# RWKV-7 time mixing: a pair's decays and scaled operands made at the end of the preceding block, and the next pair's projections ahead of the gate and v

## The chip, the cores and the metric

The kernel runs on one core of one Trainium2 chip, as one launch. The metric is the device time of that launch in microseconds, from runs on the chip; a profile was taken of one further execution. PE, DVE, ACT, POOL and SP are the core's engines for matmuls, for elementwise work, for activations, for general work and for issuing transfers; PEld is PE's loading of weights, which overlaps its matmuls.

## The reference

One inference step of a trunk with two layers, D = 1024, for a prompt of 256 tokens and for eight samples of four tokens. Layer 0 mixes tokens with Mamba-2, layer 1 with RWKV-7. What matters here is the RWKV-7 mixer:

```python
def rwkv7_mixer(u, S0, shift0, ...):
    xx = u_prev - u                                    # token shift
    xr, xw, xk, xv, xa, xg = u + xx * mu[i]            # six mixes
    r, k, v = xr @ w_r, xk @ w_k, xv @ w_v             # 1024 x 1024 each
    w = -softplus(-(w0 + tanh(xw @ w1) @ w2)) - 0.5
    a = sigmoid(a0 + (xa @ a1) @ a2)
    g = sigmoid(xg @ g1) @ g2
    kk = k * k_k, normalised per head;  k = k * (1 + (a - 1) * k_a)
    decay = exp(-exp(w))
    def step(S, inp):                                  # 16 heads of 64
        sa = S @ (-kk_t)
        S = S * d_t + sa (x) (kk_t * a_t) + v_t (x) k_t
        return S, S @ r_t
    y = groupnorm(y per head) * gn_w + gn_b + (sum(r * k * r_k) * v)
    return (y * g) @ w_o, S_new, ...
```

All of it is in float32, with the states of the recurrence as further outputs.

## The kernel before, in words

Activations lie feature-major: a tile is [128 features, 288 tokens], the 256 of the prompt and the 32 of the samples, and eight tiles are one row of 1024 features. A float32 product by a large weight is made as three matmuls (`mm3`: L147, L148, L149): weight and activation are each split into a high and a low part (`whi`, `wlo` in L55 and L56 for weights; L138 and L156, the helper `hilo`, for activations), and high x high, high x low and low x high are summed in one bank of PSUM. Weights come as 512 KB units of eight 128 x 128 tiles through two streams whose order is that in which the code asks for tiles: `ws`, whose tiles are split, and `wn`, whose tiles are used whole, as float32, by plain matmuls (L1053 in the lead, L1082 for the gate, L1132 for k). Such a matmul shows in the profile as two records.

The stage of the RWKV mixer lies at about 979 to 1300 us. Its 16 heads are worked in eight pairs (`KD = 8`), a pair being one tile of 128 features. After `lead` (norm, token shift, first half of the decays) and `bulk(0)` (projections of pair 0) it runs nine blocks, p = 0 to 8. In a block three sequences of steps are drawn in turns:

- `chain(p-1)`, in blocks 1 to 8: the recurrence of the pair before. It opens with the bonus (L1372 to L1384, two matmuls by `ones_m` in L1187 and L1188), goes through four chunks of 64 tokens and the samples in steps `solve` (L1393 to L1404), `solved` (L1409, L1410) and `state` (L1421 to L1429), and ends with the group norm, the bonus and the gate (L1470 to L1488).
- `prep(p)`, in blocks 0 to 7: the scaled operands of pair p and the inverse that `chain` needs. It has 18 steps. The first two make the decays `E1`, `E2` and `Ex` from a scan over the logarithms (L1229), the normalised key (a sum of squares by the matmuls L1187 and L1188), and the products `AR` and `BK`, which are r, k and kk times decays, padded for the samples (L1209, L1211). They begin with the load of the samples' state, `S0`, 256 KB, on SP. The third step multiplies BK by AR (L1263) and masks the result (L1269) into `AA`; the others transpose BK, and build the inverse by doubling levels (L1307 on PE, L1323 on DVE), X0, R (L1354) and TT (L1358).
- `fill(p)`: projections. `gates` (block 0 only) is the gate's first half, 16 matmuls L1082. `bulk2(p)` is the gate's second half and the v projection of pair p, with its transposes (L1178). `bulk(p+1)` is what pair p+1 needs first: sw and sa (L1098, L1099, each with a sigmoid that starts in L1119), the k projection (eight L1132) and the r projection (24 matmuls of `mm3`). In block 0 each projection also makes its mixes (L1105), and for r and v their splits. In blocks 7 and 8 come output projections (`wo`), of which `EARLY = 3` are begun in block 7.

Per round, each of `chain` and `prep` does one step and `fill` does `RATE` of its steps on average. This sets the program order. The scheduler that builds the instruction streams starts from that order and moves what its own estimate of times finds ready, so an engine's order is not the code's; the pieces of order below are what it makes of either code.

PSUM has eight banks, dealt out in rings: `main` is banks 0, 1 and 7, for projections; `A` is banks 2 and 3, for `prep` and the transposes of v; `R` is 4 and 5 and `Y` is 6, for `chain`. The products of L1263 write two banks of A for one pair of masks, and then two more for the transposes of BK. `AR` exists twice, by the parity of p; `BK` once.

After the blocks, the last of the eight terms of every output projection is added, which needs the last pair's y.

Of the kernel before, what the change touches and what calls it, by code (L numbers as in the profile page):

```python
# [16 lines left out]
KD = 8  # L17
# [8 lines left out]
class Stream:  # L26
# [34 lines left out]
    def next(self, name, kt, mt):  # L61
        self.order.append((name, kt, mt))
        self.ahead(self.k.la_split, self.k.la_units)
        i, o = divmod(self.used, PT)
        hi, lo = self.pieces[i]
        self.used += 1
        return hi[:, o * P:(o + 1) * P], lo[:, o * P:(o + 1) * P]
# [878 lines left out]


KAPPA = float(np.exp(-0.5))
RATE = 1.45
EARLY = 3  # L950
LEVELS = (1, 2, 4, 8, 16, 32)

# [539 lines left out]
def rwkv(k, g, g_next):  # L1492
    k.side = 0
    nc, ws = k.nc, k.ws
    r = k.r_next
    with k.tc.tile_pool(name="rwkv", bufs=1) as pool:
        k.wn.pool, k.wn.bufs = pool, 2
        w = Rwkv(k, pool)
        k.set_rings(main=[0, 1, 2, 3, 4, 5, 6, 7])
        w.lead(g, r)  # L1500
        w.consts()
        w.pads()
        k.set_rings(main=[0, 1, 7], A=[2, 3], R=[4, 5], Y=[6])
        for _ in w.bulk(0):
            pass
        k.renew(40, 48, F32)
        w.yg = k.A[40:48]
        ys = {}

        def wo(mo, kts):  # L1510

            ps = k.bank("main")[:, :NT]
            for i, kt in enumerate(kts):
                if kt not in ys:
                    ys[kt] = k.A[2 * kt], k.A[2 * kt + 1]
                    k.hilo(*ys[kt], w.yg[kt])
                k.mm3(ps, ws.next("r_wo", kt, mo), ys[kt], i == 0, i == len(kts) - 1)
                yield
            nc.vector.tensor_tensor(k.h[mo], k.h[mo], ps, ALU.add)

        def fill(p):

            if p == 0:
                yield from w.gates()
            if p < KD:
                yield from w.bulk2(p)
            if p + 1 < KD:
                yield from w.bulk(p + 1)
            if p == KD - 1:
                k.renew(0, 16)  # L1530
                for mo in range(EARLY):
                    yield from wo(mo, range(KD - 2))
            if p == KD:
                k.set_rings(main=[0, 1, 2, 3, 7], R=[4, 5], Y=[6])
                for mo in range(EARLY, KD):
                    yield from wo(mo, range(KD - 1))
                for mo in range(EARLY):
                    yield from wo(mo, [KD - 2])

        for p in range(KD + 1):  # L1540
            gens, acc = [], 0.0
            bulk = fill(p)
            if p < KD:
                gens.append(w.prep(p))
            if p > 0:
                gens.insert(0, w.chain(p - 1))
            while gens:
                for q in list(gens):
                    if next(q, "end") == "end":
                        gens.remove(q)  # L1550
                acc += RATE
                while acc >= 1:
                    acc -= 1
                    next(bulk, None)
            for _ in bulk:
                pass
        k.set_rings(main=[0, 1, 2, 3, 4, 5], aux=[6, 7])
        last = [wo(mo, [KD - 1]) for mo in range(KD)]
        for i in last[:6]:
            next(i)  # L1560
        k.side = 1
        k.renew(32, 48)
        for mo in range(KD):
            next(last[mo], None)
            if mo + 6 < KD:
                next(last[mo + 6])
            k.h_done(mo, g_next)
# [186 lines left out]
```

## Time and profile before

| | |
|---|---|
| runs | 1545.33, 1544.91, 1544.76 us; median 1544.91 |
| profiled execution | 1545.45 us, span of the trace 1543.6 us |
| instructions in the trace | 35587, of them 14178 matmul records on PE |
| mean granted clock of PE | 0.997 |
| L147, L148, L149 on activations and split weights | 2760 records each, 825.0, 819.0 and 814.9 us busy |
| L1132, k projections | 128 records, 40.8 us |
| L1323, masks of the inverse's levels | 40 instructions, 17.5 us of DVE |
| loads of `S0` | 8, of 256 KB, 3.7 us from issue to landing |

A page of the profile has busy times of the engines over the whole span, the chain of work that ended last, followed back from the last instruction, and groups of equal instructions with their count, busy time, mean and the idle time just ahead of them. Matmuls are pipelined, so a record's duration is longer than the distance to the next one; where the prediction speaks of the pace of matmuls, it takes distances of starts. The granted clock is a share of PE's full clock.

### The profile page before, as it was taken

What the parts mean: (1) busy time and instruction counts of PE and PEld (TensorE: products, weight loads), DVE (VectorE), ACT (ScalarE), POOL (GpSimd) and SP (SyncE); (2) the same over time, 40 slices, a digit from 0 to 9 for tenths busy, and PEclk for the clock granted to TensorE, in tenths of its full rate; (3) what the DMA queues carried; (4) which work ended last, traced back from release to release, by engine and by line L of the source; (5) the groups of instructions that cost most, each with busy time, mean ns of one, the idle gap of its engine ahead of it and who ended that gap; (6) DMA issues with size and microseconds to landing.
All of it is one profiled execution on the core that took longest, in us unless ns stands there. A gap on an engine that the chain in (4) does not pass through costs nothing.

```text
span 1543.6 us, 35587 instructions
## 1 busy us (share of the span) xinstructions
PE 1524.0 (99%) x14178; PEld 1422.4 (92%) x14178; DVE 1099.9 (71%) x2321; ACT 972.9 (63%) x2217; POOL 46.0 (3%) x143
## 2 busy tenths in 40 slices
PE   9999999999999999999999999999999999999997
PEld 8999998989989999999999999777777778999997
DVE  7666578888888766656876655887766778666566
ACT  7555458989887655554755554766666746555545
POOL 0000003112100000000000000100000000000000
PEclk9999999999999999999999999999999999999999
DMA  7555563765665555555555555531222224555551
GB/s 245 168 169 166 164 213 116 248 221 198 228 223 197 171 166 165 166 168 171 161 170 168 168 164 164 178 109 59 78 84 65 63 72 153 170 168 165 164 168 57
DMA packets 75574, 243.48 MB, mean 158 GB/s; under 512 B 11728, under 2 KB 16976, under 8 KB 75408
## 3 DMA queue, kind: packets, MB, share of 16 engines
q1 hardware_dynamic: 75408, 241.21, 48.6%
q8 instruction: 111, 1.82, 0.5%
q14 instruction: 55, 0.45, 0.1%
HBM read 226.54 MB, written 14.64 MB: 156 GB/s over the span
## 4 chain that ended last, share of the span: by engine, by line
PE 93%; DVE 4%; DMA 1%; ACT 1%; issue 1%; SPq 0%; POOL 0%; DVEq 0%; POOLq 0%; ACTq 0%
PE bank L147 26%; PE bank L149 26%; PE bank L148 25%; PE bank L1307 2%; PE bank L1132 1%; PE bank L770 1%; PE bank L1449 1%; PE bank L1421 1%; PE bank L774 1%; PE bank L766 1%; PE bank L641 1%; PE bank L1187 1%; DVE wlo L56 1%; PE bank L1381 1%; PE bank L1082 0%
## 5 line engine op out<-in xcount | busy, mean ns | idle before, releaser
L147 PE MATMUL bank<-act,whi 128*128 128x288 f32 x2760 | 825.0, 300 | 6.2 <-ACT act L138 3.7
L148 PE MATMUL bank<-act,whi 128*128 128x288 f32 x2760 | 819.0, 297 | 1.3 <-DVE act L156 1.3
L149 PE MATMUL bank<-act,wlo 128*128 128x288 f32 x2760 | 814.9, 296 | 0.1
L55 ACT ACTIVATE whi<-raw 128x512 fp32r<-128x512 f32 x754 | 472.1, 631 | 434.6 <-PE bank L148 421.9
L56 DVE TENSOR_TENSOR wlo<-raw,whi 128x512 fp32r<-128x512 f32 x754 | 515.2, 689 | 263.5 <-ACT whi L55 236.6
L147 PEld LDWEIGHTS bank<-act,whi 128*128 128x128 f32 x2760 | 517.2, 188 | 15.1 <-ACT act L138 5.2
L148 PEld LDWEIGHTS bank<-act,whi 128*128 128x128 f32 x2760 | 521.6, 189 | 6.4 <-DVE act L156 2.1
L149 PEld LDWEIGHTS bank<-act,wlo 128*128 128x128 f32 x2760 | 520.9, 189 | 3.0 <-DVE wlo L56 0.3
L147 PE MATMUL bank<-more,whi 128*128 128x288 f32 x192 | 56.7, 295 | 0.0
L148 PE MATMUL bank<-more,whi 128*128 128x288 f32 x192 | 56.4, 294 | 0.0
L149 PE MATMUL bank<-more,wlo 128*128 128x288 f32 x192 | 56.4, 294 | 0.0
L321 DVE TENSOR_TENSOR t<-bank,rstd 128x288 f32<-128x288 f32 x88 | 39.8, 456 | 23.0 <-PE bank L149 23.0
L324 DVE TENSOR_TENSOR u<-bank,s 128x288 f32<-128x288 f32 x88 | 39.8, 456 | 22.7 <-PE bank L149 22.6
L671 DVE SCALAR_TENSOR_TENSOR conv_a<-X,vec,conv_a 128x312 f32<-128x312 f32 x96 | 50.9, 534 | 2.6 <-ACT conv_a L138 2.2
L138 ACT ACTIVATE s<-t 128x288 f32<-128x288 f32 x104 | 45.8, 443 | 6.2 <-DVE t L366 3.5
L138 ACT ACTIVATE X<-bank 128x256 f32<-128x256 f32 (+2 forms) x98 | 30.5, 338 | 21.8 <-PE bank L1307 20.8
L138 ACT ACTIVATE act<-h,vec 128x288 fp32r<-128x288 f32 (+1 forms) x71 | 37.1, 528 | 7.3 <-DMA h<-in_xT 2.7
L1132 PE MATMUL bank<-act,raw 128*128 128x288 f32 x128 | 40.8, 434 | 0.0
L148 PEld LDWEIGHTS bank<-more,whi 128*128 128x128 f32 x192 | 36.3, 189 | 0.0
L149 PEld LDWEIGHTS bank<-more,wlo 128*128 128x128 f32 x192 | 36.2, 189 | 0.0
L147 PEld LDWEIGHTS bank<-more,whi 128*128 128x128 f32 x192 | 36.0, 187 | 0.0
L1323 DVE TENSOR_TENSOR Z<-bank,lv 128x256 f16<-128x256 f32 (+1 forms) x40 | 17.5, 437 | 24.1 <-PE bank L1307 23.5
(383 smaller groups left out, 1736.8 us busy)
## 6 DMA issues: line engine op xcount, KB each, us to landing
raw<-in_w SPq DMA_DIRECT2D x377, 512.0 KB, 3.6
h0a<-in_ssm_a SPq DMA_DIRECT2D x16, 512.0 KB, 5.4
h0b<-in_ssm_b SPq DMA_DIRECT2D x16, 512.0 KB, 5.1
out_ssm_s<-h0b SPq DMA_DIRECT2D x16, 512.0 KB, 3.9
raw<-in_wn SPq DMA_DIRECT2D x11, 512.0 KB, 3.6
S<-in_wkv_in SPq DMA_DIRECT2D x8, 256.0 KB, 3.7
out_wkv_s<-S SPq DMA_DIRECT2D x8, 256.0 KB, 2.0
h<-in_xT SPq DMA_DIRECT2D x8, 144.0 KB, 4.6
```

What stands on the lines that cost most here:

```text
L55: nc.scalar.activation(hi, src, AF.Copy)
L56: nc.vector.tensor_tensor(lo, src, hi.bitcast(F32), ALU.subtract)
L138: i = self.nc.scalar.activation(out, in_, func, **kw)
L147: nc.tensor.matmul(ps, wh, xh, start=start, stop=False)
L148: nc.tensor.matmul(ps, wh, xl, start=False, stop=False)
L149: nc.tensor.matmul(ps, wl, xh, start=False, stop=stop)
L321: nc.vector.tensor_tensor(t, pg, r, ALU.mult)
L324: nc.vector.tensor_tensor(u, pu, s, ALU.mult)
L671: nc.vector.scalar_tensor_tensor(a[:, :312], X[:, t:t + 312], k.g(f"conv_w{t}")[:, ct:ct + 1], a[:, :312], ALU.mult, ALU.add)
L1132: self.nc.tensor.matmul(ps, k.wn.next_whole("r_wk", kt, p), x[kt], start=kt == 0, stop=kt == KD - 1)
L1307: nc.tensor.matmul(ps[rows, ch], lhs(ch)[rows], rhs(ch)[rows], start=True, stop=True)
L1323: nc.vector.tensor_tensor(Z[:, :n], pz, lv(i, n), ALU.mult)
```

## The change

`fill` draws `bulk(p+1)` first, then in block 0 the gates, then `bulk2(p)`. `prep(p+1)` is begun in block p: as soon as `prep(p)` has ended and the r projection of pair p+1 exists (more of `fill` is drawn until it does), its first two steps run (`SCALES = 2`), and block p+1 goes on with its third. `RATE` goes from 1.45 to 1.65.

```diff
-RATE = 1.45
+RATE = 1.65
+SCALES = 2
...
         def fill(p):
 
+            if p + 1 < KD:
+                yield from w.bulk(p + 1)
             if p == 0:
                 yield from w.gates()
             if p < KD:
                 yield from w.bulk2(p)
-            if p + 1 < KD:
-                yield from w.bulk(p + 1)
...
+        def solve(p, bulk):
+
+            if p < KD:
+                yield from preps[p]
+            if p + 1 < KD:
+                while "r" not in w.d.get(p + 1, {}):
+                    next(bulk)
+                preps[p + 1] = w.prep(p + 1)
+                for _ in range(SCALES):
+                    next(preps[p + 1])
+                    yield
+
+        preps = {0: w.prep(0)}
         for p in range(KD + 1):
             gens, acc = [], 0.0
             bulk = fill(p)
-            if p < KD:
-                gens.append(w.prep(p))
+            gens.append(solve(p, bulk))
             if p > 0:
                 gens.insert(0, w.chain(p - 1))
```

Behind this place every line number is larger by one in the changed kernel: L1263 is L1264 there. No engine that computes gets more or fewer instructions; SP has one fewer, 1001 for 1002.

Four places show how the order of the engines changes. A row is a line of the code, an operation, what it writes and reads with the buffers' numbers, the shape, and how many such instructions follow one another.

PE in block 0, ahead of the first products of pair 0 (the first L1263). Before, `bank_1275` is the r projection of pair 0, `bank_1303` and `bank_1304` are the gate, `bank_1385` is sw of pair 1:

```order
L149 MATMUL bank_1275_13655<-act_1267_13611,wlo_13355 128x288
L147 MATMUL bank_1275_13655<-act_1268_13612,whi_13354 128x288
L1082 MATMUL bank_1303_13754<-mg_13781,raw_13480 128x288
L148 MATMUL bank_1275_13655<-act_1205_13441,whi_13354 128x288
L149 MATMUL bank_1275_13655<-act_1268_13612,wlo_13355 128x288
L1082 MATMUL bank_1304_13755<-mg_13781,raw_13480 128x288
L1098 MATMUL bank_1385_14155<-lw_13458,whi_13681 128x288
L1099 MATMUL bank_1385_14155<-lw_13458,wlo_13682 128x288
L1082 MATMUL bank_1303_13754<-mg_13807,raw_13480 128x288
L1082 MATMUL bank_1304_13755<-mg_13807,raw_13480 128x288
L1187 MATMUL bank_1402_14278<-ch_14279,ones_m_13570 128x288
L1263 MATMUL bank_1312_13787<-AR_1249_13589,BK_13591 64x128
```

In the changed order `bank_1329` is the r projection of pair 1, `bank_1310` its k projection (whose L1132 is now L1133), and the gate's matmuls come behind:

```order
L147 MATMUL bank_1329_13914<-act_1263_13607,whi_13378 128x288
L148 MATMUL bank_1329_13914<-act_1200_13436,whi_13378 128x288
L149 MATMUL bank_1329_13914<-act_1263_13607,wlo_13379 128x288
L147 MATMUL bank_1329_13914<-act_1264_13608,whi_13378 128x288
L1133 MATMUL bank_1310_13789<-act_1253_13597,raw_13480 128x288
L1133 MATMUL bank_1310_13789<-act_1254_13598,raw_13480 128x288
L1133 MATMUL bank_1310_13789<-act_1255_13599,raw_13480 128x288
L1133 MATMUL bank_1310_13789<-act_1256_13600,raw_13480 128x288
L1133 MATMUL bank_1310_13789<-act_1257_13601,raw_13480 128x288
L1264 MATMUL bank_1313_13796<-AR_1249_13589,BK_13591 64x128
L1264 MATMUL bank_1314_13797<-AR_1249_13589,BK_13591 64x128
```

What moved: the gate's L1082 are gone from here, and projections of pair 1 stand in their place.

PE in block 4, from the last products of BK and AR (ring A, both banks) to the next products that need a bank of ring A:

```order
L1263 MATMUL bank_1780_16208<-AR_1249_13589,BK_13591 64x128
L1263 MATMUL bank_1781_16209<-AR_1249_13589,BK_13591 64x128
L1409 MATMUL bank_1794_16325<-rhs_16287,TT_16097 64x64 x2
L1409 MATMUL bank_1796_16332<-rhs_16294,TT_16097 64x64 x2
L1132 MATMUL bank_1825_16481<-act_1255_13599,raw_15259 128x288
L1263 MATMUL bank_1784_16247<-AR_1249_13589,BK_13591 64x64 x2
L1263 MATMUL bank_1784_16247<-r_const_13561,BK_13591 64x64 x7
L1263 MATMUL bank_1785_16248<-AR_1249_13589,BK_13591 64x64 x2
```

The same stretch in the changed order:

```order
L1264 MATMUL bank_1774_16186<-AR_1249_13589,BK_13591 64x128
L1264 MATMUL bank_1775_16187<-AR_1249_13589,BK_13591 64x128
L1396 MATMUL bank_1794_16309<-S_16290,AR_1250_13590 64x64 x2
L1398 MATMUL bank_1794_16309<-SAV_16122,AA_15571 64x64 x2
L1402 MATMUL bank_1770_16165<-AR_1250_13590,S_16290 64x64 x2
L1394 MATMUL bank_1796_16318<-r_const_13561,q_16182 64x64 x2
L1398 MATMUL bank_1796_16318<-SAV_16122,AA_15571 64x64 x2
L1264 MATMUL bank_1782_16227<-AR_1249_13589,BK_13591 64x64 x2
L1264 MATMUL bank_1782_16227<-r_const_13561,BK_13591 64x64 x7
L1264 MATMUL bank_1783_16228<-AR_1249_13589,BK_13591 64x64 x2
```

Between the two groups of products stood two `solved` and one matmul of a k projection; now one `solve` and the samples' `solve` stand there.

DVE in block 4, up to the masks of pair 4 (L1269; `AA`). Before, the scaled products of pair 4 are made here, beside steps of chain 3:

```order
L1119 TENSOR_SCALAR sw_16435<-bank_1815_16432,vec_129 128x288
L1251 TENSOR_TENSOR rs_q_16145<-rs_q_16145,sa_15836 128x288
L1404 TENSOR_SCALAR rhs_16287<-bank_1786_16280 128x64
L1209 TENSOR_TENSOR BK_13591<-rs_q_16145,ss_16159 128x4x64
L1211 TENSOR_TENSOR BK_13591<-rs_q_16145,ss_16159 128x8x4
L1404 TENSOR_SCALAR rhs_16294<-bank_1788_16289 128x64
L1119 TENSOR_SCALAR sa_16447<-bank_1817_16440,vec_129 128x288
L56 TENSOR_TENSOR wlo_16670<-raw_15737,whi_16669 128x512
L56 TENSOR_TENSOR wlo_16718<-raw_15737,whi_16717 128x512
L1269 TENSOR_TENSOR AA_16206<-bank_1780_16208,r_const_13561 128x512
L1269 TENSOR_TENSOR AA_16206<-bank_1781_16209,r_const_13561 128x512
```

In the changed order:

```order
L1405 TENSOR_SCALAR rhs_16225<-bank_1780_16222 128x64
L1252 TENSOR_TENSOR rs_q_16102<-rs_q_16102,sa_15606 128x288
L1411 COPY SAV_16122<-bank_1785_16262 64x64
L1210 TENSOR_TENSOR BK_13591<-rs_q_16102,ss_16116 128x4x64
L1212 TENSOR_TENSOR BK_13591<-rs_q_16102,ss_16116 128x8x4
L1120 TENSOR_SCALAR sa_16217<-bank_1778_16214,vec_129 128x288
L1425 TENSOR_SCALAR S_16290<-bank_1790_16287,E_1641_15502 128x64
L56 TENSOR_TENSOR wlo_16698<-raw_15905,whi_16697 128x512
L1270 TENSOR_TENSOR AA_16184<-bank_1774_16186,r_const_13561 128x512
L1270 TENSOR_TENSOR AA_16184<-bank_1775_16187,r_const_13561 128x512
```

The products of pair 4 stand ahead of its masks by about as many rows as before; chain 3 has moved: its `solved` (L1411) and the state it makes (L1425) now come in this stretch, its two `solve` before and after it. The first product of r (`AR` from `r` and `E`, then L1209, now L1210) stood 30 rows ahead of the first mask and stands 39 ahead.

PE at the end of the stage, from the last matmul by `ones_m` in the last chain (L1188) on; all of it but that row are output projections of earlier pairs:

```order
L1188 MATMUL bank_2276_18851<-cl_18841,ones_m_13570 128x288
L149 MATMUL bank_2280_18894<-act_2170_18269,wlo_18801 128x288
L147 MATMUL bank_2280_18894<-act_2172_18271,whi_18800 128x288
L148 MATMUL bank_2280_18894<-act_2173_18272,whi_18800 128x288
L149 MATMUL bank_2280_18894<-act_2172_18271,wlo_18801 128x288
L147 MATMUL bank_2280_18894<-act_2174_18273,whi_18800 128x288
L148 MATMUL bank_2280_18894<-act_2175_18274,whi_18800 128x288
L149 MATMUL bank_2280_18894<-act_2174_18273,wlo_18801 128x288
L147 MATMUL bank_2280_18894<-act_2176_18275,whi_18800 128x288
L148 MATMUL bank_2280_18894<-act_2177_18276,whi_18800 128x288
L149 MATMUL bank_2280_18894<-act_2176_18275,wlo_18801 128x288
L147 MATMUL bank_2280_18894<-act_2178_18277,whi_18830 128x288
```

In the changed order, up to the first output projection that needs the last pair, the last row here:

```order
L1189 MATMUL bank_2277_18866<-cl_18854,ones_m_13570 128x288
L147 MATMUL bank_2281_18923<-act_2178_18286,whi_18824 128x288
L148 MATMUL bank_2281_18923<-act_2179_18287,whi_18824 128x288
L149 MATMUL bank_2281_18923<-act_2178_18286,wlo_18825 128x288
L147 MATMUL bank_2282_18932<-act_2178_18286,whi_18824 128x288
L148 MATMUL bank_2282_18932<-act_2179_18287,whi_18824 128x288
L149 MATMUL bank_2282_18932<-act_2178_18286,wlo_18825 128x288
L147 MATMUL bank_2283_18939<-act_2178_18286,whi_18824 128x288
L148 MATMUL bank_2283_18939<-act_2179_18287,whi_18824 128x288
L149 MATMUL bank_2283_18939<-act_2178_18286,wlo_18825 128x288
L147 MATMUL bank_2284_18944<-act_2180_18288,whi_18859 128x288
```

Before, eleven more such matmuls follow the rows shown until the first one that needs the last pair, 22 in all; now it is nine.

## The prediction

> **What bounds the kernel now.** I read the page first: the span, the busy shares, and the chain of work that ended last.
>
> ```profile
> span 1543.6 us, 35587 instructions
> PE 1524.0 (99%) x14178; PEld 1422.4 (92%) x14178; DVE 1099.9 (71%) x2321; ACT 972.9 (63%) x2217; POOL 46.0 (3%) x143
> PE 93%; DVE 4%; DMA 1%; ACT 1%; issue 1%; SPq 0%; POOL 0%; DVEq 0%; POOLq 0%; ACTq 0%
> ```
>
> PE is the bound: 93% of the chain. A change of order can therefore win only what PE spends idle, at half clock, or on changing between full-array and smaller matmuls. Next I cut the RWKV stage into stretches: lead and first operands, rest of block 0, blocks 1 to 7, block 8 and what follows it. The columns after the window are its length and then the busy time of PE, weight load, DVE and ACT.
>
> ```profile
> 979.00:1012.00 33.00, 29.01 (x176) 20.92 (x177) 32.40 (x87) 23.04 (x73) 6.33 (x18) 0.95 0.46 151
> 1012.00:1044.00 32.00, 31.91 (x401) 25.23 (x397) 25.05 (x65) 24.08 (x64) 0.00 (x0) 1.00 0.33 108
> 1044.00:1262.00 218.00, 215.81 (x3283) 160.32 (x3283) 158.03 (x434) 142.75 (x393) 0.00 (x0) 1.00 0.23 72
> 1262.00:1300.00 38.00, 36.53 (x359) 31.02 (x358) 28.59 (x71) 19.37 (x47) 0.00 (x0) 0.96 0.36 109
> ```
>
> Two regimes: up to 1012 DVE is busy 32.4 of 33 us and PE waits 4 us for it; from then on PE is busy 99% and little is left to win. What PE waits for between 979 and 1300 us (total, times, longest), and below it one row of the weight loads, where the same wait looks longer because a matmul's end is modelled:
>
> ```profile
> PE bank L147 <- ACT act L138: 3.7, 3, 1.5
> PE bank L1263 <- DVE AA L1269: 2.1, 6, 0.6
> PE bank L148 <- DVE act L156: 0.9, 3, 0.4
> ...
> PEld bank L1263 <- DVE AA L1269: 4.5, 7, 1.0
> ```
>
> The rows on `act` are the operand splits of the first r projection (2.4 of the 3.7, and the 0.9 of L148) and of the last output projection (1.3, shown under term 5). The L1263 row comes once a block, and it is the only one at the place where the scaled operands are used.
>
> **The change, part by part.** It removes and adds no instruction on any engine that computes: the same work in another order. Five terms.
>
> *1. Fewer changes of array form.* The price is in the PE timeline of a middle block.
>
> ```profile
> 1127.33 0.29 PE L147 MATMUL bank<-act,whi 128*128 128x288 f32 x1
> 1127.46 0.29 PE L148 MATMUL bank<-act,whi 128*128 128x288 f32 x1
> 1127.68 0.31 PE L1307 MATMUL bank<-Z,XT 64*64 64x64 f16 x8
> 1127.83 0.29 PE L1307 MATMUL bank<-XT,Z 64*64 64x64 f16 x8
> 1128.05 0.40 PE L1187 MATMUL bank<-ch,center 128*128 128x288 f32 x1
> 1128.29 0.29 PE L149 MATMUL bank<-act,wlo 128*128 128x288 f32 x1
> ```
>
> Full matmuls start 0.13 us apart; the last one before small ones takes 0.22 (+0.09), the first one after them 0.24 (+0.11), and the second eight small ones hold PE 0.22 where the first eight held it 0.15 (+0.07). A stay in the small form so costs 0.27 us beyond its work. Counted over the two orders, from L1053 to the last L1188, PE leaves the full array 189 times before and 181 times now: 8 x 0.27 = 2.2 us won. The stays differ in what they hold, so I allow 1 us either way.
>
> *2. The scaled operands in the preceding block.* That step issues, per pair, the S0 load on SP, two L1187/L1188 matmuls on PE, nine activations (kk, two squares, E1, E2, Ex, Ln, Exp, t) and 16 DVE instructions (L1195, the scan L1229, six sums and products from L1234 to L1251, four pairs of padded products in L1209 and L1211). None is dropped. In block p the scaling of pair p+1 now runs beside the end of chain p-1, instead of in block p+1 beside the beginning of chain p. On SP the load moves past a few weight loads, but its buffer is freed by the write of S0 in the middle of the same block and it is read only in the next one; I cost it at nothing, cover some 20 us. What it should relieve is the L1263 wait. So I looked at what that wait waits for.
>
> ```profile
> 1144.18 0.28 PE L1263 MATMUL bank<-AR,BK 64*64 64x128 f32 x2
> ...
> 1144.41 0.75 PE L1132 MATMUL bank<-act,raw 128*128 128x288 f32 x2
> ...
> 1144.61 1.28 DVE L1269 TENSOR_TENSOR AA<-bank,r_const 128x512 f32<-128x512 f32 x2
> ...
> 1145.34 0.33 PE L1263 MATMUL bank<-AR,BK 64*64 64x64 f32 x4 [0.18 <-DVE AA L1269]
> ```
>
> It is not operands. The first 16 products of BK and AR fill both banks of ring A; the next ones need the same banks, and go on when the first of the two masks on DVE is through, 0.73 us after it began and about 0.88 after the products ended. Earlier operands do not shorten that. What fills it is what stands between on PE: in the middle blocks four small products (L1409) and one L1132 before, ten small products of a solve now. By the rows that is 0.3 us less cover in three blocks, against two blocks with seven or more matmuls there and more cover. I take 0 for all; ends: all of it goes (-2.1 by PE, -4.5 by weight loads) or cover is lost in every block (7 x 0.3 = +2.1).
>
> This reading is also that of the Trainium skill, "Perfetto Trace Analysis", section Optimization Strategy: a gap that repeats over a stretch on the saturated engine can mean that there is no SBUF or PSUM buffer for the next tile. By that rule, which speaks against this change, the term is 0; by the plain reading of the wait as one for operands it is -2.1. The trace agrees with the rule, by the bank that both products write.
>
> *3. Block 0, up to the first masks.* DVE sets the pace here:
>
> ```profile
> 991.00:1003.40 12.40, 9.09 (x36) 6.58 (x36) 12.18 (x29) 10.08 (x27) 4.43 (x14) 0.86 0.29 101
> 1003.40:1012.30 8.90, 8.43 (x103) 5.88 (x102) 8.74 (x25) 2.22 (x5) 0.00 (x0) 1.00 0.31 103
> L1105 DVE SCALAR_TENSOR_TENSOR t<-act,vec,act 128x288 f32<-128x288 f32 x10 | 4.8, 508 | 0.0
> L156 DVE TENSOR_TENSOR act<-t,act 128x288 fp32r<-128x288 f32 x10 | 4.6, 463 | 0.2 <-ACT act L138 0.2
> L56 DVE TENSOR_TENSOR wlo<-raw,whi 128x512 fp32r<-128x512 f32 x3 | 2.0, 682 | 0.0
> L1229 DVE TENSOR_TENSOR_SCAN rs_y<-scan,sw 128x288 f32<-128x288 f32 x1 | 0.7, 744 | 0.0
> 1003.23 0.65 PE L1082 MATMUL bank<-mg,raw 128*128 128x288 f32 x2
> ```
>
> Between the first L1119 and the second mask the DVE order has 47 instructions before and 47 now: out go six mixes (6 x 0.48 = 2.9) and an L156 (0.46); in come three weight splits (3 x 0.67 = 2.0), two first steps of sigmoids (1.0, priced like the mixes), a scan (0.74) and an L1372 (0.46). So the masks come 0.9 us later. By then PE has done more: 22 gate matmuls are out and 16 of k are in, both of the form of the last row (two in 0.65, the second 0.25 after the first), so -1.5; 19 more projection matmuls at 0.13 (+2.5) and one or two single ones (+0.1). That is 1.1 us of work in advance for 0.9 of delay: -0.2.
>
> *4. v at the end of block 0.* The mixes and splits for v now stand after the gates: 8 x (0.48 + 0.46) = 7.5 us of DVE for 24 x 0.13 = 3.1 us of PE. The rest, 4.4 us, is covered only because the order puts the next pair's r projection (24 matmuls, 3.1 us) and the end of pair 0's inverse (three levels, X0 and R, some 3 us) between. I cost it at 0; if that cover fails it is +4.4.
>
> *5. The end of the stage.* RATE draws the output projections of block 8 forward, away from the last chain's end.
>
> ```profile
> 1287.51 0.29 PE L1188 MATMUL bank<-cl,ones_m 128*128 128x288 f32 x1
> 1287.64 0.29 PE L149 MATMUL bank<-act,wlo 128*128 128x288 f32 x1
> ...
> 1290.44 0.29 PE L149 MATMUL bank<-act,wlo 128*128 128x288 f32 x1
> 1292.08 1.06 PE L147 MATMUL bank<-act,whi 128*128 128x288 f32 x6 [1.34 <-ACT act L138]
> ```
>
> From the last L1188 the norm, the gate and the split take 4.57 us until the first dependent L147. Before, 22 projections stand in that gap and 1.3 us stay idle; now nine do. The 13 that left, 13 x 0.13 = 1.7 us, are done earlier, where PE had hardly a gap (the 38 us window above has 36.5 busy, and 1.3 of the rest is this very wait). So +1.7.
>
> The sum: -2.2 + 0 - 0.2 + 0 + 1.7 = -0.7 us. The profiled execution took 1545.45 us, span 1543.6 and 1.85 around it, so it would take 1544.75; it lies 0.54 above the median of the three runs, and on that median I forecast **1544.2 us**.
>
> **Rivals.**
>
> *Faster: the blocks close up.* If the operands, and not the banks, hold L1263, because the masks themselves are delayed on DVE by the scaling that stands ahead of them, then moving it frees the wait in all seven blocks: between 2.1 and 4.5 us, 3.3 in the middle. For it: the longest of these waits is 0.6 and the one shown 0.18, so there may be something besides the bank. Against: DVE still has a sum, a weight split and part of the next scan there. 1544.2 - 3.3 = 1540.9 us, and 1539.7 if all 4.5 go.
>
> *Slower: v uncovered.* The fourth term at +4.4: 1548.6. For it: the first r projection, the same pattern, cost PE 2.4 + 0.9 us in waits. Against: the 6 us of other work.
>
> *Slower: half clock at the block ends.* The columns as in the windows above; the seventh is the granted clock.
>
> ```profile
> 1260.00:1263.40 3.40, 3.40 (x86) 2.78 (x81) 1.94 (x7) 2.52 (x8) 0.00 (x0) 1.00 0.44 154
> 1263.40:1266.80 3.40, 3.40 (x28) 2.71 (x28) 2.28 (x5) 1.72 (x5) 0.00 (x0) 0.50 0.00 0
> 1263.81 0.44 PE L148 MATMUL bank<-act,whi 128*128 128x288 f32 x1
> 1264.05 0.44 PE L149 MATMUL bank<-act,wlo 128*128 128x288 f32 x1
> ```
>
> After a stretch of 3.4 us with 86 mostly small matmuls the clock was 0.50 for the next 3.4 us, and full matmuls started 0.24 apart instead of 0.13. With nine of them that costs 1.0 us, and 0.2 for the small ones. It happened once, in block 7's end. Now chain start (L1381), X0, L1352 and R stand together in every block, with L1132 between; if blocks 1 to 6 each lose a window, 6 x 1.2 = +7.2 us: 1551.4. It decides from four windows up. Against: the L1132 between are full matmuls of the long form.
>
> The Trainium skill, "TensorE: Matmul & The Clock Gate", section Why this matters for your kernels, asks for idle gaps of more than about 3 us before the clock falls. By that rule this rival could not happen, since PE had no such gap from 1260 to 1263; the row shows half clock all the same, so here the measurement decides.
>
> **How the numbers follow.** My forecast 0.52, the blocks close up 0.27, v uncovered 0.13, half clock 0.08. A measurement of this kernel tells about 0.2%, 3.1 us, from no change. Faster by more (under 1541.8): the first rival, 0.27. Slower by more (over 1548.0): the last two and a little of the forecast, 0.23. Within: 0.50. The range goes from the first rival with the whole wait, 1539.5, to v uncovered with a little more, 1549.0, and leaves out the half clock in many blocks and less than that on the other side. The likeliest case alone: 1542 to 1547.
>
> **What would show it.** Term 1: PE's busy time from 1044 to 1262, less by 1 to 2 us. Term 2: the row L1263 <- DVE AA again with 1.5 to 3 us; if it is gone, the first rival holds. Term 3: masks of block 0 at about 1013. Term 4: a wait of L147 on `act` near 1035; over 2 us means the second rival. Term 5: a wait of about 3 us, instead of 1.3, ahead of the first dependent L147. Half clock: windows with a granted clock below 1 between 1044 and 1262, none before. What would make it wrong: DVE or ACT late in a block's last third, where chain end, inverse end and scaling now meet, as waits of L1307 or L1397 on PE.

## The result, and the profile after

The changed kernel is slower, by less than 1%: 1556.46 us (median of 4 runs, 1555.61 to 1558.04) against 1544.84 us (median of 4 runs shown beside them), a ratio of 1.0077 with a 95% interval of 1.0059 to 1.0094. The forecast was 1544.2 us in a range of 1539.5 to 1549.0, so it missed by 12.3 us and the range by 7.5. Ratios here and below leave out slow executions, of which there was one: 2809.2 us, at a mean clock of 0.948, among the ten of RATE 1.65 alone. The profiled execution took 1555.61 us, and its page begins:

```profile
span 1553.7 us, 35628 instructions
PE 1533.4 (99%) x14178; PEld 1431.7 (92%) x14178; DVE 1100.5 (71%) x2321; ACT 973.2 (63%) x2217; POOL 48.0 (3%) x143
PE 93%; DVE 3%; DMA 1%; ACT 1%; issue 0%; SPq 0%; POOL 0%; DVEq 0%; POOLq 0%; ACTq 0%
```

PE is the bound as before, with the same 14178 records, but it is busy 9.4 us longer. The same matmuls took longer: PE ran at a lower clock (mean granted clock 0.991, before 0.997). In the RWKV stage the trace has stretches of 6.83, 13.65 and 3.41 us at half clock, where before had two of 3.41; the 17.1 us more are worth up to 8.5 us.

Where it happened is read from a landmark that both kernels have once per pair, TT, the end of a pair's inverse. These are the rows of that line in two windows, before and after (after the counts and durations, the starts of the first and the last): pairs 0 and 1, and pairs 1 to 6.

```profile
L1358 DVE TENSOR_TENSOR TT<-bank,XT x2: 423/424/424, 1034.3 to 1071.6; 128x256 f32<-128x256 f32 x2
L1358 DVE TENSOR_TENSOR TT<-bank,XT x6: 423/423/424, 1071.6 to 1235.8; 128x256 f32<-128x256 f32 x6
```

```profile
L1359 DVE TENSOR_TENSOR TT<-bank,XT x2: 424/424/425, 1033.5 to 1079.4; 128x256 f32<-128x256 f32 x2
L1359 DVE TENSOR_TENSOR TT<-bank,XT x6: 423/425/425, 1079.4 to 1244.0; 128x256 f32<-128x256 f32 x6
```

Up to pair 0's TT the changed kernel is 0.8 us ahead. From there to pair 1's it takes 45.9 us where it took 37.3: +8.6. The five blocks from pair 1 to 6 take 164.6 for 164.2, and the rest of the span 309.7 for 307.8: +1.9. The loss is one place, with a smaller one at the stage's end.

At that place, the windows of the changed kernel (columns as in the prediction; the last three are granted clock, DMA share, GB/s) and one of before over the same microseconds:

```profile
1026.00:1037.70 11.70, 11.14 (x150) 9.14 (x150) 8.37 (x22) 9.52 (x25) 0.00 (x0) 1.00 0.17 49
1037.70:1041.13 3.43, 1.79 (x9) 0.94 (x7) 3.43 (x11) 1.56 (x4) 0.00 (x0) 1.00 0.39 143
1041.13:1054.78 13.65, 13.13 (x80) 9.59 (x80) 7.48 (x18) 6.30 (x17) 0.00 (x0) 0.50 0.20 60
```

```profile
1037.70:1041.10 3.40, 3.40 (x25) 2.84 (x25) 2.37 (x7) 1.50 (x5) 0.00 (x0) 1.00 0.26 86
```

PE is busy 1.79 of 3.43 us while DVE is busy all the time, and then the granted clock is 0.50 for 13.65 us. PE's timeline there:

```profile
1037.91 0.30 PE L1100 MATMUL bank<-lw,wlo 128*128 128x288 f32 x1
1039.04 0.40 PE L147 MATMUL bank<-act,whi 128*128 128x288 f32 x1 [0.84 <-ACT act L138]
1040.02 0.40 PE L148 MATMUL bank<-act,whi 128*128 128x288 f32 x1 [0.58 <-DVE act L156]
1040.26 0.29 PE L149 MATMUL bank<-act,wlo 128*128 128x288 f32 x1
1040.47 0.43 PE L1264 MATMUL bank<-AR,BK 64*64 64x128 f32 x2
1041.36 0.61 PE L147 MATMUL bank<-act,whi 128*128 128x288 f32 x1 [0.46 <-ACT act L138]
1042.02 1.12 PE L1264 MATMUL bank<-AR,BK 64*64 64x128 f32 x8
1043.71 0.44 PE L147 MATMUL bank<-act,whi 128*128 128x288 f32 x1
1043.95 0.44 PE L148 MATMUL bank<-act,whi 128*128 128x288 f32 x1
```

These L147 to L149 are the v projection of pair 0. PE waits 0.84, 0.58 and 0.46 us for its operands, and from 1041 on two full matmuls start 0.24 us apart, not 0.13. DVE in the same microseconds shows why the operands are late:

```profile
1036.88 0.45 DVE L156 TENSOR_TENSOR act<-t,act 128x288 fp32r<-128x288 f32 x1
1037.25 0.42 DVE L1210 TENSOR_TENSOR BK<-k,ss 128x256 f32<-128x256 f32 x1
1037.58 0.51 DVE L1106 SCALAR_TENSOR_TENSOR t<-act,vec,act 128x288 f32<-128x288 f32 x1
1038.01 0.18 DVE L1212 TENSOR_TENSOR BK<-k,ss 128x32 f32<-128x32 f32 x1
1038.12 0.51 DVE L1248 SCALAR_TENSOR_TENSOR rk<-r,vec,k 128x288 f32<-128x288 f32 x1
1038.55 0.45 DVE L1250 TENSOR_TENSOR rs_q<-rs_q,s 128x288 f32<-128x288 f32 x1
1038.91 0.68 DVE L56 TENSOR_TENSOR wlo<-raw,whi 128x512 fp32r<-128x512 f32 x1
1039.52 0.45 DVE L156 TENSOR_TENSOR act<-t,act 128x288 fp32r<-128x288 f32 x1
```

Two splits of v (L156) lie 2.64 us apart; one of the six instructions between them is v's next mix (L1106), four belong to pair 1's scaled operands and one is a weight split. At the stage's end:

```profile
1300.85 0.61 PE L147 MATMUL bank<-act,whi 128*128 128x288 f32 x1 [3.14 <-ACT act L138]
```

```profile
1300.55:1303.96 3.41, 3.11 (x13) 3.11 (x14) 1.67 (x4) 1.03 (x4) 0.00 (x0) 0.50 0.87 268
```

The wait of 1.34 us has become 3.14, and a stretch at half clock follows it.

### The profile page after: what moved, and what is told of

It is laid out like the page before. It is cut to its first block, busy times and chain, and to the rows that moved or that the text cites. A ratio compares the mean times of both kernels' runs of the same rounds, so it can differ in the third digit from the quotient of the medians.

```text
span 1553.7 us, 35628 instructions
## 1 busy us (share of the span) xinstructions
PE 1533.4 (99%) x14178; PEld 1431.7 (92%) x14178; DVE 1100.5 (71%) x2321; ACT 973.2 (63%) x2217; POOL 48.0 (3%) x143
## 4 chain that ended last, share of the span: by engine, by line
PE 93%; DVE 3%; DMA 1%; ACT 1%; issue 0%; SPq 0%; POOL 0%; DVEq 0%; POOLq 0%; ACTq 0%
PE bank L147 26%; PE bank L149 25%; PE bank L148 25%; PE bank L1308 2%; PE bank L1133 2%; PE bank L1264 1%; PE bank L770 1%; PE bank L1450 1%; PE bank L774 1%; DVE wlo L56 1%; PE bank L766 1%; PE bank L1422 1%; PE bank L641 1%; PE bank L1188 1%; PE bank L1382 1%
## 5 line engine op out<-in xcount | busy, mean ns | idle before, releaser
L147 PE MATMUL bank<-act,whi 128*128 128x288 f32 x2760 | 828.6, 301 | 6.5 <-ACT act L138 5.7
L149 PE MATMUL bank<-act,wlo 128*128 128x288 f32 x2760 | 817.1, 296 | 0.1
L147 PEld LDWEIGHTS bank<-act,whi 128*128 128x128 f32 x2760 | 518.8, 188 | 16.7 <-ACT act L138 8.2
L149 PEld LDWEIGHTS bank<-act,wlo 128*128 128x128 f32 x2760 | 522.2, 189 | 3.5 <-DVE wlo L56 0.4
L147 PE MATMUL bank<-more,whi 128*128 128x288 f32 x192 | 56.7, 295 | 0.0
L149 PE MATMUL bank<-more,wlo 128*128 128x288 f32 x192 | 56.4, 294 | 0.0
L1133 PE MATMUL bank<-act,raw 128*128 128x288 f32 x128 | 39.9, 430 | 0.0
L149 PEld LDWEIGHTS bank<-more,wlo 128*128 128x128 f32 x192 | 36.2, 189 | 0.0
L147 PEld LDWEIGHTS bank<-more,whi 128*128 128x128 f32 x192 | 36.0, 187 | 0.0
```

The source lines that it names most:

```text
L147: nc.tensor.matmul(ps, wh, xh, start=start, stop=False)
L149: nc.tensor.matmul(ps, wl, xh, start=False, stop=stop)
L1133: self.nc.tensor.matmul(ps, k.wn.next_whole("r_wk", kt, p), x[kt], start=kt == 0, stop=kt == KD - 1)
```

## The experiments

Theory A: v of pair 0, drawn behind pair 1's projections, comes when nothing is left to cover its operands; PE idles, the clock falls to half, and that is the loss. Rivals: B, the moved scaling costs in every block; C, RATE.

**Block 0 in the old order.** Everything else as changed.

```diff
         def fill(p):
+            if p == 0:
+                yield from w.gates()
+                yield from w.bulk2(p)
             if p + 1 < KD:
                 yield from w.bulk(p + 1)
-            if p == 0:
-                yield from w.gates()
-            if p < KD:
+            if 0 < p < KD:
                 yield from w.bulk2(p)
```

> The changed kernel, but block 0 draws its projections in the old order (gates, then g and v, then the next pair's); blocks 1 to 7, SCALES and RATE stay as changed. Theory A (v of pair 0 comes late: its mixes and splits meet the scaled operands of pair 1 on DVE, PE idles there, and the clock falls to half for 13.65 us): the half clock near 1041 us is gone and most of the 9 us lost between 1034 and 1057 us come back, 1546 to 1549 us, with the wait of about 3 us at the stage's end still there. Theory B (the loss is in all blocks, from the moved scaling): 1553 us or more. Theory C (RATE): no change from 1556.

Measured: 1544.39 us, ratio to before 0.9993 (0.9984 to 1.0003). 12 us come back, the half clock at 1041 is gone, and the end of the stage still has a wait of 3.1 us. Without block 0's new order nothing is lost; B and C fall as the cause. The gain was 3 us more than theory A had priced, and the time lies below its range. Pairs 1 to 6 in this kernel:

```profile
L1359 DVE TENSOR_TENSOR TT<-bank,XT x6: 425/425/426, 1067.4 to 1230.8; 128x256 f32<-128x256 f32 x6
```

From the stage's first L1054 to pair 1's TT it takes 87.0 us (from 980.4) and the changed kernel 100.5 (from 978.9). Both do 126 projection matmuls there, the kernel before 137 in 92.1 us. Against a kernel with as many projections up to that point the new order of block 0 so costs 13.5 us; theory A's 9 came from the comparison with before, which had more to do there. Of the 13.5, 17.1 us more at half clock (20.5 for 3.4) are up to 8.5; the rest is not taken apart.

**The order of projections alone**, in every block (no early scaled operands, RATE 1.45).

> The kernel before with the new order of projections in every block, but without the early scaled operands, and RATE 1.45. Theory A as a matter of v alone: the half clock after about 1037 us is there, and +7 to +9 us. Theory A as a matter of the crowd (v's mixes and pair 1's scaling together on DVE): PE idles less at v, no long half clock, +1 to +4 us. In this order no output projection stands between the last chain's last matmul and the first projection that needs it, so the wait at the stage's end should be about 4.3 us instead of 1.3, under every theory. 1548 (crowd) against 1556 (v alone).

Measured: 1561.73 us, ratio 1.0108 (1.0093 to 1.0123), worse than either expectation. The clock is at half for 10.24 us behind v, and the wait at the end is 3.7 us. Up to pair 1's TT it takes 100.7 us for 126 projections, as the changed kernel does, so `SCALES` is not needed for that loss. But this does not take the scaled operands away from v. DVE at v in this kernel:

```profile
1040.33 0.46 DVE L156 TENSOR_TENSOR act<-t,act 128x288 fp32r<-128x288 f32 x1
1040.70 0.94 DVE L1105 SCALAR_TENSOR_TENSOR t<-act,vec,act 128x288 f32<-128x288 f32 x2
1041.56 0.42 DVE L1209 TENSOR_TENSOR BK<-k,ss 128x256 f32<-128x256 f32 x1
1041.89 0.18 DVE L1211 TENSOR_TENSOR BK<-k,ss 128x32 f32<-128x32 f32 x1
1042.00 0.51 DVE L1247 SCALAR_TENSOR_TENSOR rk<-r,vec,k 128x288 f32<-128x288 f32 x1
1042.42 0.82 DVE L156 TENSOR_TENSOR act<-t,act 128x288 fp32r<-128x288 f32 x2
```

The products of pair 1 (L1209 to L1247) stand between v's splits here too, since v now comes so late that it meets them at the start of pair 1's own block. So the runs cannot tell v alone from v beside this scaling. The five blocks behind it:

```profile
L1358 DVE TENSOR_TENSOR TT<-bank,XT x6: 417/424/425, 1079.6 to 1249.9; 128x256 f32<-128x256 f32 x6
```

They take 170.3 us, 6.1 more than before, but 41 more projections lie in that stretch (302 for 261), 5.3 us of work at 0.13 each that other stretches then lack. Whether this order has a second cost in the blocks is not shown by that row.

**The early scaled operands alone** (old order everywhere, RATE 1.45).

> The changed kernel with the old order of projections in every block and RATE 1.45: the early scaled operands alone. Theory A: v is early, no half clock near 1041 us, 1544 to 1549 us, with nine projections over the last chain's end and a wait of about 3 us there. Theory B (the moved scaling itself costs): 1550 us or more, lost in steps of about 1 us per block.

Measured: 1542.63 us, ratio 0.9983 (0.9974 to 0.9993): faster than before, and below the range of theory A. Rows of TT and of PE's waits between 979 and 1300 us:

```profile
L1359 DVE TENSOR_TENSOR TT<-bank,XT x2: 424/424/425, 1035.8 to 1072.1; 128x256 f32<-128x256 f32 x2
L1359 DVE TENSOR_TENSOR TT<-bank,XT x6: 424/425/425, 1072.1 to 1230.0; 128x256 f32<-128x256 f32 x6
```

```profile
PE bank L147 <- ACT act L138: 5.6, 3, 3.1
PE bank L1264 <- DVE AA L1270: 0.5, 1, 0.5
```

Five blocks take 157.9 us for 164.2, the opposite of B. The end of the stage gives part of it back: a wait of 3.1 us and 6.83 us at half clock behind it.

**RATE 1.65 alone.**

> The kernel before with RATE 1.65 alone. The prediction put the thinner cover at the stage's end down to RATE; the order of this kernel has 22 projections there, as before. So the wait there should be 1.3 us as before and the time 1544 to 1546 us. Theory C (RATE has a part in the loss): 1548 us or more.

Measured: 1544.26 us, ratio 0.9995 (0.9985 to 1.0005), wait at the end 1.3 us. RATE does nothing that can be told here.

**Block 0 in the new order alone** (the complement of the first run: all else as before).

> The kernel before with the new order of projections in block 0 alone: pair 1's projections, then the gate, then g and v of pair 0; no early scaled operands, RATE 1.45. Theory A (the late v of pair 0 is the loss, whatever else is changed): PE idles ahead of v's operands near 1040 us, half clock for two to four stretches of 3.41 us, 7 to 9 us lost between the ends of the inverses of pairs 0 and 1, 1552 to 1555 us. Theory A' (it takes the early scaled operands of pair 1 on DVE beside v): no long half clock there, 1546 to 1548 us.

Measured: 1551.61 us, ratio 1.0038 (1.0025 to 1.0051), between the two expectations. PE's windows in block 0's end:

```profile
1029.15:1032.56 3.41, 2.59 (x50) 1.76 (x44) 1.47 (x5) 1.88 (x6) 0.00 (x0) 1.00 0.30 121
1032.56:1039.39 6.83, 6.55 (x46) 5.38 (x47) 5.88 (x16) 4.68 (x11) 0.00 (x0) 0.50 0.01 2
```

The clock does fall, but a little ahead of v's late operands: behind a window in which PE did mostly small matmuls of the inverse and waited for the gate, with no projection left to stand between. At half clock PE then hardly waits for v (0.2 us). Pair 0's TT to pair 1's takes 41.2 us, 3.9 more than before and not 8.6. The half clock begins ahead of the first of the two; from the first L1053 to pair 1's TT it is 96.3 us for 92.1, with 134 projections for 137. Another part is a wait of 2.8 us at the stage's end with 6.83 us at half clock behind it. So the new order of block 0 costs by itself, less than theory A said; in the changed kernel the place lost twice as much. The early scaling is not what tells them apart, since the new order in every block lost as much without it, and products of pair 1 stand beside v here too (L1209 at 1041.57). There the half clock lasted 10.24 us at v and here 6.83. Why it lasted longer, no run settles. Nor does a run move v alone: the new order moves the gate with it.

**PE fed at v.** The changed kernel with matmuls that nobody reads.

```diff
+        if p == 0 and n == "v":
+            self.idle = k.bank("main")[:, :NT]
         for kt in range(KD):
             if p == 0:
                 self.mix(i, kt, x)
+                if n == "v":
+                    for _ in range(4):
+                        nc_ = self.nc
+                        nc_.tensor.matmul(self.idle, self.ones_m, self.lgh, start=True, stop=True)
```

> The changed kernel, and ahead of each of the eight steps of pair 0's v projection four more matmuls of 128 x 288 on a bank that nobody reads: 32 matmuls of added work, 32 x 0.13 = 4.2 us at full clock. Theory A1 (PE's idling ahead of v's operands makes the clock fall, and the half clock for 13.65 us is most of the loss): PE is fed there, the half clock at 1041 us is gone or shorter, and the time falls in spite of the added work: 1556.5 - 6.8 + 4.2 - about 2 of filled waits, 1550 to 1554 us. Theory A2 (the loss is the waiting for DVE; the half clock costs little since PE waits anyway): the added work costs its time less the filled waits, 1557 to 1561 us.

Measured: 1551.82 us, ratio to before 1.0042 (1.0028 to 1.0056); 4.2 us of added work made the changed kernel 4.6 us faster. The windows:

```profile
1037.70:1041.10 3.40, 3.40 (x21) 2.66 (x20) 3.40 (x12) 1.92 (x5) 0.00 (x0) 1.00 0.00 0
1041.10:1054.80 13.70, 13.70 (x142) 10.59 (x142) 9.87 (x22) 9.51 (x23) 0.00 (x0) 1.00 0.32 95
```

DVE is as busy as it was (3.40 of 3.40), PE no longer idles, and the clock stays full: 142 matmuls in the time in which the changed kernel did 80. This is what theory A1 expected. One thing moved besides: k matmuls of pair 2 also came into the gap, so not all of the feeding is the added work.

**Three banks in ring A.** Before, with `main=[0, 1], A=[2, 3, 7]`.

> The kernel before with three banks in ring A and two in ring main. If the wait of L1263 for the masks is one for a bank of ring A, as the prediction says, its row (2.1 us, 6 times) shrinks to one product's bank, 0.5 us or less, or is gone. If it is one for operands or for DVE's order, it stays at 1.5 us or more. The time says little, since ring main has one bank fewer.

```profile
PE bank L1263 <- DVE AA L1269: 2.0, 6, 0.6
```

The row did not shrink, so the expectation failed. But the run does not decide it: the first of the next two products now has a bank, the second needs the bank of the first mask, and the order put nothing but the first one's eleven matmuls between. The early scaled operands alone say more. PE and DVE in a middle block of that kernel:

```profile
1141.37 1.09 PE L1264 MATMUL bank<-AR,BK 64*64 64x128 f32 x28
1142.85 0.75 PE L1133 MATMUL bank<-act,raw 128*128 128x288 f32 x2
1143.64 0.33 PE L1264 MATMUL bank<-AR,BK 64*64 64x64 f32 x4
```

```profile
1142.92 1.26 DVE L1270 TENSOR_TENSOR AA<-bank,r_const 128x512 f32<-128x512 f32 x2
```

The next products still begin just when the first of the two masks is through (1142.92 + 0.63 = 1143.55), 0.09 us later. It is no longer a wait because solves and a k matmul fill the 1.3 us between. That fits a bank; it is argued from times, not shown by taking the bank away.

**The end of the stage**, on the early scaled operands alone. First EARLY 2, then EARLY 1 with RATE 1.2 in block 8, then EARLY 2 with 13 matmuls that nobody reads ahead of the last output projections.

> The early scaled operands alone (old order of projections, RATE 1.45), with EARLY 2 instead of 3, so that one more output projection is left to block 8. In its order 19 projections stand over the last chain's end, where the early scaled operands alone have nine. If the wait of 3.1 us there and the half clock of 6.83 us behind it are what is left to win: wait 3.1 - 10 x 0.13 = 1.8 us, no or one half clock window, 1537 to 1541 us, against 1542.6. If that wait is not worth its time: 1542 to 1543.

> The early scaled operands alone, with EARLY 1 and RATE 1.2 in block 8: in its order 24 projections stand over the last chain's end, where EARLY 2 has 19. If cover of that end is what counts: a wait of 1.75 - 5 x 0.13 = 1.1 us, below the 1.3 us behind which the kernel before shows no half clock, so none here: 1541.3 - 0.65 - up to 1.7 = 1539 to 1540.7 us. If block 7, which has 12 projections fewer to fill its gaps, then waits instead: 1541 to 1543 us.

> The early scaled operands alone with EARLY 2, and 13 matmuls on a bank that nobody reads at the one place where PE waits for the last chain's end (13 x 0.13 = 1.7 us of added work in a wait of 1.75 us). If PE's idling there makes the clock fall to half for the 3.41 us after it: no half clock there, and up to 1.7 us faster than the same kernel without them (1541.3), 1539.6 to 1540.5 us. If the half clock has another cause: 1541.3 to 1541.6, half clock as before.

Measured: 1541.30 us, ratio 0.9976 (0.9967 to 0.9985); 1540.84 us, 0.9961 (0.9948 to 0.9973); 1540.74 us, 0.9965 (0.9952 to 0.9979). The waits at the end are 1.7, 1.4 and none, near what was expected; each time lies 0.1 to 0.3 us above its range. Windows at the end of the first and of the third:

```profile
1284.88:1288.29 3.41, 1.67 (x12) 1.42 (x11) 2.79 (x8) 1.07 (x2) 0.00 (x0) 1.00 0.43 147
1288.29:1291.70 3.41, 3.41 (x16) 3.41 (x15) 3.41 (x9) 2.94 (x8) 0.00 (x0) 0.50 0.90 255
```

```profile
1284.00:1288.30 4.30, 4.30 (x33) 4.08 (x31) 3.52 (x9) 2.88 (x6) 0.00 (x0) 1.00 0.38 122
1288.30:1291.70 3.40, 3.40 (x27) 3.37 (x26) 2.77 (x9) 1.85 (x5) 0.00 (x0) 1.00 0.72 207
```

With PE fed, 27 matmuls instead of 16 are done in the stretch behind the wait: the half clock there does come from PE's idling. The three times lie too close for an order among them; all beat both kernels.

**PE fed at the first r projection too.**

> The same as the last, and 21 more matmuls on a bank that nobody reads between the steps of pair 0's r projection, where PE waits 2.4 + 0.9 us for operands from DVE and the clock is half for 3.41 us or more in every kernel so far (2.7 us of added work at full clock). DVE sets the pace there, so a faster PE wins little: 0 to 1.5 us faster than the last if the half clock goes, and 1 us slower if the added work outlasts the waits.

Measured: 1541.82 us, ratio 0.9977 (0.9968 to 0.9986). Every other profile here has a stretch at half clock between 992 and 1007 us; this one has none:

```profile
996.60:1003.80 7.20, 6.76 (x42) 5.61 (x40) 7.20 (x20) 6.07 (x16) 0.00 (x0) 1.00 0.18 64
```

The time did not fall. DVE is busy 7.20 of 7.20 there, which fits that it sets the pace. But the time alone does not price the clock at this place: from the stage's first matmul to block 0's first mask it takes 30.3 us, without this feeding 31.4, and the same profile has 6.83 us at half clock at 1130.33, where the other has 3.41 at 1102.43.

## Why the prediction was wrong, by its steps

*Term 4, v at the end of block 0: costed at 0, measured about +9 us against before, and +13.5 against the kernel with block 0 in the old order.* This is the step that failed, and twice. First, the cover it named did not last: in the timeline the next pair's r projection and pair 0's inverse are over by 1035.9, while v's splits come until 1047, with pair 1's scaled operands between them. Term 2 had counted those 16 DVE instructions, but in the middle blocks only, never in block 0 beside v. Second, the rival "v uncovered" priced the failure by DVE time alone, +4.4. The waits cost only some 2.3 us (0.20 + 0.84 + 0.58 + 0.46 and 0.25 for a mask); 13.65 us at half clock cost up to 13.65 / 2 = 6.8. Together 9.1, against 8.6 between the two rows of TT (and 0.8 more if the six full matmuls that the stretch has fewer than before are counted). The sign set for it, over 2 us of L147's wait on `act` near 1035, stayed silent: 0.84 and 0.46 are 1.3 us. The two rivals that the text kept apart, uncovered operands and half clock, were one mechanism here: the first brought the second.

*Rival half clock.* It was put at the ends of the blocks and given 0.08. In the changed kernel's trace no such stretch lies between 1055 and 1300 us; it came at the idle places instead. The measurement differs from the rule of the Trainium skill ("TensorE: Matmul & The Clock Gate", section Why this matters for your kernels) even where PE idles: no single gap from 1037.70 to 1041.13 is longer than 0.84 us, far below the 3 us it names, and the clock fell. At the stage's end, behind the gap of 3.14 us, the trace agrees with it.

*Term 1, the array form: -2.2.* The mechanism fits and the size was of the right order, but the change hardly uses it in the blocks. Its sign failed: PE is busy 216.6 us from 1052 to 1270, before 215.8 in the same length from 1044. Counted in the traces from pair 1's TT to pair 6's, PE leaves the full array 111 times before, 108 in the changed kernel, 90 with the early scaled operands alone and 129 with the new order alone. Full projection matmuls in that stretch are 261, 272, 253 and 302. For the early scaled operands: 157.9 - 164.2 = -6.3, and 8 projections more would be 1.0, so -5.3; PE's waits give 1.7 of it (L1263 for the mask, before; none now). If all the rest is put down to the 21 stays, it is 3.6 / 21 = 0.17 us each (prediction: 0.27). Corrected in the same way, the changed kernel's +0.4 is -1.0 (11 projections more) and the new order's +6.1 is +0.8. So most of what the early scaled operands win in the blocks by themselves is missing beside the new order, with 108 stays for 90.

*Term 2, the wait of L1263: 0.* About right for the changed kernel: L1264 still waits 1.5 us, 5 times, for the mask. The rival "the blocks close up" has the right outcome for the early scaled operands alone; that wait is 1.7 us of their 5.3.

*Term 3, block 0 up to the masks: -0.2.* From the first L1053 to pair 0's TT the kernels take 54.8 and 54.6 us, and the first mask starts 0.9 us later (1010.15 and 1011.03), as worked out. That the first agrees to 0.2 us is in part luck: the stretch now holds six projections fewer and 6.83 us at half clock instead of 3.41.

*Term 5, the end: +1.7.* The wait was forecast at about 3 us and is 3.14; the rest of the span is 1.9 longer. The cause given, RATE, is wrong: RATE alone leaves the cover of 22 projections, and the early scaled operands at RATE 1.45 have nine. The 3.41 us at half clock behind the wait were not foreseen, and the rest of the span before had such a stretch too, at 1263.40, which the changed kernel lacks: that the size came out is in part luck.

## What to carry to other kernels

When work is moved ahead of something whose operands another engine makes, list everything else that engine has to do in those microseconds; the first time round a loop is its own case, since it has work that the middle blocks don't have. Price a PE wait in the middle of a saturated kernel with the half clock that can follow it, up to three times the wait itself here. And try the halves of a change apart: here one half is worth -2.5 us alone, -4 with the end mended, and was buried under the other. Before a stretch between two landmarks is compared in two orders, count the work that lies in it.

## What the runs showed of the hardware

The half clock comes in whole pieces: 3.41, 6.83, 10.24 and 13.65 us. A long gap is not needed ahead of one: two came behind a window of 3.41 us with few matmuls, 9 records (after, 1037.70) and 12 (1284.88 above), and with no gap over 0.84 and 1.74 us. This window of before, with 16 records and 1.34 us of idling, was followed by full clock:

```profile
1290.70:1294.11 3.41, 2.07 (x16) 2.00 (x16) 3.39 (x9) 1.13 (x3) 0.00 (x0) 1.00 0.58 183
```

The count of records is no border, though: with block 0 in the old order a window of 9 records, PE busy 2.30 of 3.41 us from 992.37, was also followed by full clock, and only the next, with 8, by half. Half clock can also follow windows in which PE never idles but does mostly small matmuls, as here at EARLY 2, near the end of a pair's inverse:

```profile
1192.72:1196.13 3.41, 3.41 (x57) 2.67 (x55) 2.25 (x7) 2.63 (x8) 0.00 (x0) 1.00 0.37 137
1196.13:1199.54 3.41, 3.41 (x37) 2.95 (x36) 1.33 (x4) 1.61 (x4) 0.00 (x0) 0.50 0.00 0
```

Such a stretch was in the profile of before at 1263.40, with EARLY 1 at 1164.02 and 1228.88, in the two fed kernels of EARLY 2 at 1102.43 and 1130.33, and in the changed kernel nowhere in the blocks. Runs of one kernel differ in how much half clock they have: at EARLY 2 the run with a mean clock of 0.997 took 1539.16 us and that with 0.990 took 1546.56; where in those runs it fell was not profiled.
